# A norm's squares added over partitions by two float32r matmuls, and 1/rms by a root, a reciprocal and a Newton step

## The chip, the cores and the metric

The kernel runs on one core of one Trainium2 chip. The metric is device time in microseconds (us) of one execution, as the median of several runs. The program is one hybrid decoder layer, float32 in and out.

## What is computed

With 256 tokens and a model width of 1024, the part that matters is the second half of the layer:

```
x   = x + mixed @ w_out                     # residual, x is (256, 1024)
h2  = x * rsqrt(mean(x*x over 1024) + 1e-6) * norm_ffn_g
up  = causal_depthwise_conv(h2 @ w_up, conv_w, conv_b)    # 3 taps along tokens
gate, val = split(up, 2)                    # 2816 each
out = x + (silu(gate) * val) @ w_down
```

Ahead of it stand a first norm, eight heads of attention, a pooling branch and two gated branch projections. They are not touched.

## The kernel before

Everything after the projections for q, k and v lies transposed: features on the 128 partitions, the 256 tokens along the row. A feature tile is 128 features, so x has 8 tiles (`xT[:, j, :]`), and the FFN has 22 gate tiles and 22 value tiles.

**Split products.** A float32 matmul is replaced by three float32r ones. Every weight and every activation is split into a high part, rounded by ScalarE (ACT), `high` (L84, L85), and a low part, the difference, made by VectorE (DVE), `low` (L87 to L91). `mm3` (L93) multiplies high by high, high by the activation's low part, and the weight's low part by high. A product of 8 feature tiles is thus 24 matmuls of 128x128 by 128x256.

**Weights.** They come as chunks of 128x2048 floats, in one list (`order`, L102 to L112): up25 is the FFN's tile 0 (one gate tile and one value tile), up26 tile 1, up27 tile 2, up28 tile 3, dn29 two tiles of the down projection, up30 tile 4, up31 tile 5, dn32, and so on. SyncE loads them into 4 buffers. Each chunk is split in two halves of 128x1024: `next_high` (L145) rounds the next half on ACT, `next_low` (L159) makes the difference of an earlier one on DVE, one half behind, and then issues a load. `ahead` (L169) does one of each, and a second time if fewer low halves than `upto` are ready beyond the chunk in use. Each engine takes its instructions in the order in which the code gives them, so where a call of `ahead` stands decides what its half stands behind on ACT and on DVE. The first half of an up chunk holds feature tiles 0 to 3, the second 4 to 7; the third matmul of a feature tile reads the low half.

**The second norm.** After each output tile of `w_out`, `residual` (L588) adds it to x, splits x times the norm's weight into `hhi` and `hlo`, and adds its squares to `ss2` (128 x 256, on POOL, the last one on DVE). The norm's factor is applied after the up projection: `normed` (L630) multiplies a finished tile by `R2`, in which every partition holds 1/rms of all 256 tokens.

The code around the change is L676 to L697. The first two up tiles (up0_0 and up0_1) run over the first 7 feature tiles. Then two matmuls with `ss2` as the weights and a column of ones (L682) put the sums per token on partitions. `rms` (L250) adds epsilon on DVE and takes the power -1/2 on POOL. After the last feature tile of both, two calls of `ahead` and the third up tile (up1_0), `diagonal` (L256) puts the factors on the diagonal of two 128x128 matrices, high and low, and `spread_rms` (L263) multiplies them by `ones_r`, a matrix of ones, which puts every token's factor on all partitions; DVE copies it to `R2`. From there each tile pair goes through `normed`, `taps` (two DVE steps of the convolution), Silu on ACT and the product on POOL; `down` (L654) follows from tile 3 on, three tiles behind.

The line numbers in the profile are those of this kernel; a helper's line stands for all its callers.

Of the kernel before, what the change touches and what calls it, by code (L numbers as in the profile page):

```python
# [8 lines left out]
F32 = mybir.dt.float32  # L9
F32R = mybir.dt.float32r  # L10
AF = mybir.ActivationFunctionType
ALU = mybir.AluOpType
AX = mybir.AxisListType

P = 128
S = 256
NT = S // P
D = 1024
# [12 lines left out]
EPS = 1e-6  # L31
# [20 lines left out]
AHEAD = 4  # L52
FFN_AHEAD = 6
FIRST = 1
HOME = 8
LEAD = 104


# [6 lines left out]
def hybrid_layer_kernel(ctx: ExitStack, tc: tile.TileContext, xq_d, xtok_d, par_d, wkv_d, wpg_d,  # L65
                        wpool_d, wba_d, wbp_d, wout_d, wup_d, wdn_d, out_d):
    nc = tc.nc

    const = ctx.enter_context(tc.tile_pool(name="const", bufs=1))
# [7 lines left out]
    ps2 = pairs.enter_context(tc.tile_pool(name="ps2", bufs=2, space=bass.MemoryType.PSUM))  # L77
    tmp = mixer.enter_context(tc.tile_pool(name="tmp", bufs=2))
# [5 lines left out]
    def high(hi, src, scale=1.0):  # L84
        nc.scalar.activation(hi, src, AF.Copy, scale=scale)  # L85

    def low(lo, hi, src, scale=None):  # L87
        if scale is None:
            nc.vector.tensor_tensor(lo, src, hi.bitcast(F32), ALU.subtract)  # L89
        else:  # L90
            nc.vector.scalar_tensor_tensor(lo, src, scale, hi.bitcast(F32), ALU.mult, ALU.subtract)  # L91
# [53 lines left out]
    def next_high():  # L145
        if at[0] < len(pieces):
            c, sl, first, _ = pieces[at[0]]
            if c - oldest() >= WBUFS:
                return
            at[0] += 1  # L150
            if first:
                moving = order[c][0] in "qkv"
                place = MOVING if moving else 0
                his[c] = whi_p.tile([P, CH + P], F32R, tag="whi", name=f"hi_{order[c][0]}{c}")[:, place:]
                place = MOVING if moving else FAR
                los[c] = wlo_p.tile([P, CH + P], F32R, tag="wlo", name=f"lo_{order[c][0]}{c}")[:, place:]
            high(his[c][:, sl], raw(c, sl))

    def next_low(eager=False):  # L159
        if at[1] < at[0] - STAGGER or at[0] == len(pieces) > at[1] or (at[1] < at[0] and eager):  # L160
            c, sl, _, last = pieces[at[1]]
            at[1] += 1
            low(los[c][:, sl], his[c][:, sl], raw(c, sl))
            if last and order[c][0] != "q":
                load()
# [3 lines left out]
    def ahead(upto=0):  # L169

        next_high()
        next_low()
        if at[1] - sum(p[0] < used[0] for p in pieces) < upto:
            next_high()
            next_low()

    def chunk(name):
        c = used[0]
        used[0] += 1
        spent.update(i for i in range(c) if order[i][0] != "dn")  # L180
        assert order[c][0] == name and all(p[0] > c for p in pieces[at[1]:]), (name, order[c][0])
        return his[c], los[c]


    ones = const.tile([P, P], F32, name="ones")
    nc.vector.memset(ones, 1.0)
    ones_r = const.tile([P, P], F32R, name="ones_r")
# [9 lines left out]
    scrap = const.tile([P, 1], F32, name="scrap")  # L197
# [21 lines left out]

    ident = const.tile([P, P], F32, name="ident")  # L220
    make_identity(nc, ident)
    ss1 = const.tile([P, HOME], F32, name="ss1")[:, 0:NT]
    mhalf = const.tile([P, H], F32, name="mhalf")
    nc.gpsimd.memset(mhalf, -0.5)
    mask = const.tile([P, 3, P], F32, name="mask")
# [18 lines left out]
    R1 = const.tile([P, S], F32, name="R1")  # L244
    rtok1 = const.tile([P, NT], F32, name="rtok1")
    R2 = const.tile([P, S], F32, name="R2")
    rtok2 = const.tile([P, NT], F32, name="rtok2")
    diag = const.tile([P, 2, NT, P], F32R, name="diag")

    def rms(rtok, ss, name):  # L250

        v = const.tile([P, NT], F32, name=f"var_{name}")
        nc.vector.tensor_scalar(v, ss, 1.0 / D, EPS, op0=ALU.mult, op1=ALU.add)
        nc.gpsimd.tensor_tensor(rtok, v, mhalf[:, 0:NT], ALU.pow)

    def diagonal(rtok):  # L256

        for t in range(NT):
            high(diag[:, 0, t, :], ident, rtok[:, t:t + 1])
        for t in range(NT):  # L260
            low(diag[:, 1, t, :], diag[:, 0, t, :], ident, rtok[:, t:t + 1])

    def spread_rms(pb, R):  # L263

        for i in range(2):
            nc.tensor.matmul(pb, ones_r, diag[:, i].rearrange("p t c -> p (t c)"), start=i == 0, stop=i == 1)
        nc.vector.tensor_copy(R, pb)
# [290 lines left out]
    tmp = ctx.enter_context(tc.tile_pool(name="ffn", bufs=2))  # L558
# [18 lines left out]
    hhi = act.tile([P, KD, S], F32R, tag="xhi", name="hhi")  # L577
    hlo = act.tile([P, KD, S], F32R, tag="xlo", name="hlo")
    ss2 = tmp.tile([P, S], F32, tag="ss2", bufs=1, name="ss2")

    def tile_part(w, opers, c, ps, ks):
        hi, lo = w
        oph, opl = opers
        for k in ks:
            sl = slice(k * 256 + c * P, k * 256 + (c + 1) * P)
            mm3(ps[:, 0:S], (hi[:, sl], lo[:, sl]), (oph[:, k, :], opl[:, k, :]), k == 0, k == KD - 1)

    def residual(j, ps):  # L588
        nc.vector.tensor_tensor(xT[:, j, :], ps[:, 0:S], xT[:, j, :], ALU.add)
        g = par[:, C_FFN + j:C_FFN + j + 1]  # L590
        high(hhi[:, j, :], xT[:, j, :], g)
        if j == 0:
            nc.scalar.activation(ss2, xT[:, j, :], AF.Square)
        else:
            s2 = tmp.tile([P, S], F32, tag="s2", name=f"s2_{j}")
            nc.scalar.activation(s2, xT[:, j, :], AF.Square)
            if j < KD - 1:
                nc.gpsimd.tensor_tensor(ss2, ss2, s2, ALU.add)
        if j < KD - 2:
            ahead(AHEAD if j % 2 == 0 else 0)  # L600
        low(hlo[:, j, :], hhi[:, j, :], xT[:, j, :], g)
        if j == KD - 1:
            nc.vector.tensor_tensor(ss2, ss2, s2, ALU.add)

    nc.scalar.activation(scrap, ones[:, 0:1], AF.Silu)
    for b in range(4):
        w = chunk("o")
        ps = [bank(f"ps_out{b}{c}") for c in range(2)]
        if b == 0:

            for ks in (range(KD - 1), range(KD - 1, KD)):
                for c in range(2):
                    tile_part(w, (mh, ml), c, ps[c], ks)
            residual(0, ps[0])
            residual(1, ps[1])
        else:
            for c in range(2):
                tile_part(w, (mh, ml), c, ps[c], range(KD))
                residual(2 * b + c, ps[c])
    ahead()  # L620


    acch, accl = {}, {}

    def taps(u, f, c):
        cw = [par[:, C_CW + j * 2 * KF + f:C_CW + j * 2 * KF + f + 1] for j in range(3)]
        nc.vector.scalar_tensor_tensor(c[:, 1:S], u[:, 0:S - 1], cw[1], c[:, 1:S], ALU.mult, ALU.add)
        nc.vector.scalar_tensor_tensor(c[:, 2:S], u[:, 0:S - 2], cw[0], c[:, 2:S], ALU.mult, ALU.add)  # L628

    def normed(ps, f, name):  # L630

        u = tmp.tile([P, S], F32, tag="u", bufs=4, name=f"u_{name}")
        nc.vector.tensor_tensor(u, ps[:, 0:S], R2, ALU.mult)  # L633
        c = tmp.tile([P, S], F32, tag="cv", bufs=5, name=f"c_{name}")
        cw = par[:, C_CW + 2 * 2 * KF + f:C_CW + 2 * 2 * KF + f + 1]
        nc.scalar.activation(c, u, AF.Identity, scale=cw, bias=par[:, C_CB + f:C_CB + f + 1])
        return u, c

    def gate_done(i, uc):
        taps(uc[0], i, uc[1])  # L640
        nc.scalar.activation(uc[1], uc[1], AF.Silu)

    def value_done(i, g, uc):
        taps(uc[0], KF + i, uc[1])
        nc.gpsimd.tensor_tensor(uc[1], g[1], uc[1], ALU.mult)  # L645
        acch[i] = tmp.tile([P, S], F32R, tag="ah", bufs=LAG + 2, name=f"ah{i}")
        accl[i] = tmp.tile([P, S], F32R, tag="al", bufs=LAG + 2, name=f"al{i}")
        high(acch[i], uc[1])
        return uc[1]
# [27 lines left out]
    ps0 = [bank(f"ps_up0_{c}") for c in range(2)]  # L677
    for c in range(2):
        tile_part(w0, (hhi, hlo), c, ps0[c], range(KD - 1))
    stat = ps2.tile([P, 2, 512], F32, tag="ps2", name="ps_n2")  # L680
    for t in range(NT):
        nc.tensor.matmul(stat[:, 0, t:t + 1], ss2[:, t * P:(t + 1) * P], ones[:, 0:1], start=True, stop=True)  # L682
    rms(rtok2, stat[:, 0, 0:NT], "n2")
    for c in range(2):
        tile_part(w0, (hhi, hlo), c, ps0[c], range(KD - 1, KD))
    for _ in range(2):
        ahead()
    w = chunk("up")
    ps = [bank("ps_up1_0")]
    tile_part(w, (hhi, hlo), 0, ps[0], range(KD))  # L690
    diagonal(rtok2)
    ahead()
    spread_rms(stat[:, 1, 0:S], R2)
    ug = normed(ps0[0], 0, "g0")
    uv = normed(ps0[1], KF, "v0")
    gate_done(0, ug)
    done = value_done(0, ug, uv)  # L697
    for i in range(1, KF):
# [104 lines left out]
```

## Time and profile before

| | us |
|---|---|
| median of 3 runs | 336.04 (335.89 to 336.39) |
| the profiled execution | 336.69 |
| its span, first to last instruction | 334.9 |
| TensorE busy | 330.4 (99%) |
| VectorE busy | 257.4 (77%) |
| ScalarE busy | 201.3 (60%) |
| POOL busy | 87.6 (26%) |

The span is the stretch that the profile shows; the rest of the execution lies around it. In the profile PE is the matmuls, PEld their weight loads, which lie beside other matmuls. Durations of neighbours on PE overlap: the pace is the distance of two starts, not the duration of one. A row of the timeline gives a start, a duration, the engine, the line, and what was written from what; idle time before it stands in brackets with what ended it. Buffer numbers are left out in these names, so `lo_up` is any up chunk's low part. The granted clock of TensorE was 0.999 of full speed over the span.

### The profile page before, as it was taken

To read this page: it belongs to the slowest core of one execution; us is meant where nothing else is said; L and a number is where in the kernel's file an instruction comes from. 1 tells how busy PE (TensorE), PEld (TensorE's weight loads), DVE (VectorE), ACT (ScalarE), POOL (GpSimd) and SP (SyncE) were. 2 spreads that over 40 slices of the span, in tenths; PEclk is the share of its full clock that TensorE was granted. 3 is DMA by queue.
4 is the path that set the end of the run, shared out by engine and by line. 5 is a ranking of instruction groups with operands and counts; after the bars stand their busy time and mean duration, and the time that the engine had idled before them with its cause. 6 is when DMAs were issued, how large, how long until landed. Compare 5 with 4: busy or idle time off the path is not lost.

```text
span 334.9 us, 6726 instructions
## 1 busy us (share of the span) xinstructions
PE 330.4 (99%) x2734; PEld 321.0 (96%) x2734; DVE 257.4 (77%) x409; ACT 201.3 (60%) x325; POOL 87.6 (26%) x100
## 2 busy tenths in 40 slices
PE   8999999999999999999999999999999999999995
PEld 7888899999999999999999999999999999999995
DVE  4839999978776785898998888777778777777644
ACT  5768627654849864677566666555556564646420
POOL 1006893102404034023232312121212121212230
PEclk9999999999999999999999999999999999999999
DMA  7997653464364390573566566463736464551003
GB/s 263 421 416 290 219 183 124 153 252 133 138 232 158 131 342 2 168 248 157 197 241 213 171 245 202 179 250 128 250 130 249 144 236 158 221 174 78 0 2 125
DMA packets 10686, 63.81 MB, mean 191 GB/s; under 512 B 1184, under 2 KB 2336, under 8 KB 3616
## 3 DMA queue, kind: packets, MB, share of 16 engines
q1 hardware_dynamic: 10656, 63.39, 52.3%
q8 instruction: 21, 0.34, 0.4%
q14 instruction: 9, 0.07, 0.1%
HBM read 62.33 MB, written 1.05 MB: 189 GB/s over the span
## 4 chain that ended last, share of the span: by engine, by line
PE 97%; DMA 1%; ACT 0%; DVE 0%; issue 0%
PE ps_up L97 12%; PE ps_up L98 12%; PE ps_up L99 12%; PE ps_d L662 6%; PE ps_d L664 6%; PE ps_d L663 6%; PE ps_g L97 5%; PE ps_g L99 4%; PE ps_g L98 4%; PE ps_q L284 4%; PE ps_v L284 3%; PE ps_k L284 3%; PE ps_out L99 2%; PE ps_out L98 2%; PE ps_out L97 2%; DMA xq<-in_xq 1%
## 5 line engine op out<-in xcount | busy, mean ns | idle before, releaser
L98 PE MATMUL ps_up<-hlo,hi_up 128*128 128x256 f32 x352 | 97.3, 276 | 0.0
L97 PE MATMUL ps_up<-hhi,hi_up 128*128 128x256 f32 x352 | 97.3, 276 | 0.0
L99 PE MATMUL ps_up<-hhi,lo_up 128*128 128x256 f32 x352 | 97.2, 276 | 0.0
L98 PEld LDWEIGHTS ps_up<-hlo,hi_up 128*128 128x128 f32 x352 | 66.1, 188 | 0.1
L97 PEld LDWEIGHTS ps_up<-hhi,hi_up 128*128 128x128 f32 x352 | 66.1, 188 | 0.0
L99 PEld LDWEIGHTS ps_up<-hhi,lo_up 128*128 128x128 f32 x352 | 66.1, 188 | 0.0
L89 DVE TENSOR_TENSOR lo_up<-raw_up,hi_up 128x1024 fp32r<-128x1024 f32 x44 | 55.8, 1271 | 6.5 <-ACT hi_up L85 6.5
L662 PE MATMUL ps_d<-ah,hi_dn 128*128 128x256 f32 x176 | 48.6, 276 | 0.0
L663 PE MATMUL ps_d<-al,hi_dn 128*128 128x256 f32 x176 | 48.6, 276 | 0.0
L664 PE MATMUL ps_d<-ah,lo_dn 128*128 128x256 f32 x176 | 48.6, 276 | 0.0
L645 POOL TENSOR_TENSOR c_v<-c_g,c_v 128x256 f32<-128x256 f32 x22 | 16.2, 737 | 117.5 <-DVE c_v L628 112.1
L85 ACT ACTIVATE hi_up<-raw_up 128x1024 fp32r<-128x1024 f32 x44 | 45.1, 1046 | 0.0
L85 ACT ACTIVATE ah<-c_v 128x256 fp32r<-128x256 f32 x22 | 9.2, 418 | 45.8 <-POOL c_v L645 45.8
L97 PE MATMUL ps_g<-xhi,hi_g 128*128 128x256 f32 x128 | 35.9, 280 | 0.0
L98 PE MATMUL ps_g<-xlo,hi_g 128*128 128x256 f32 x128 | 35.3, 276 | 0.0
L99 PE MATMUL ps_g<-xhi,lo_g 128*128 128x256 f32 x128 | 35.3, 276 | 0.0
L663 PEld LDWEIGHTS ps_d<-al,hi_dn 128*128 128x128 f32 x176 | 33.0, 188 | 0.0
L664 PEld LDWEIGHTS ps_d<-ah,lo_dn 128*128 128x128 f32 x176 | 33.0, 188 | 0.0
L662 PEld LDWEIGHTS ps_d<-ah,hi_dn 128*128 128x128 f32 x176 | 33.0, 188 | 0.0
L89 DVE TENSOR_TENSOR lo_dn<-raw_dn,hi_dn 128x1024 fp32r<-128x1024 f32 x22 | 27.3, 1242 | 0.4 <-ACT hi_dn L85 0.4
L633 DVE TENSOR_TENSOR u_v<-ps_up,R 128x256 f32<-128x256 f32 x22 | 9.3, 421 | 20.5 <-PE ps_up L99 20.5
L669 POOL TENSOR_TENSOR al<-c_v,ah 128x256 fp32r<-128x256 f32 x22 | 21.5, 979 | 11.6 <-ACT ah L85 11.6
(182 smaller groups left out, 804.3 us busy)
## 6 DMA issues: line engine op xcount, KB each, us to landing
raw_up<-in_wup SPq DMA_DIRECT2D x22, 1024.0 KB, 4.8
raw_dn<-in_wdn SPq DMA_DIRECT2D x11, 1024.0 KB, 4.7
raw_g<-in_wpg SPq DMA_DIRECT2D x8, 1024.0 KB, 4.9
raw_o<-in_wout SPq DMA_DIRECT2D x4, 1024.0 KB, 4.8
raw_v<-in_wkv SPq DMA_DIRECT2D x2, 1024.0 KB, 15.7
raw_p<-in_wpg SPq DMA_DIRECT2D x2, 1024.0 KB, 11.3
raw_bp<-in_wbp SPq DMA_DIRECT2D x2, 1024.0 KB, 4.8
raw_ba<-in_wba SPq DMA_DIRECT2D x2, 1024.0 KB, 4.9
```

The costliest lines, as they stand in the source:

```text
L85: nc.scalar.activation(hi, src, AF.Copy, scale=scale)
L89: nc.vector.tensor_tensor(lo, src, hi.bitcast(F32), ALU.subtract)
L97: nc.tensor.matmul(out, sh, mh, start=start, stop=False, **kw)
L98: nc.tensor.matmul(out, sh, ml, start=False, stop=False, **kw)
L99: nc.tensor.matmul(out, sl, mh, start=False, stop=stop, **kw)
L284: nc.tensor.matmul(pt[t], sx[:, k, t * P:(t + 1) * P], wx[:, sl], start=k == 0 and sx is xhi and wx is hi, stop=k == KD - 1 and wx is lo)
L633: nc.vector.tensor_tensor(u, ps[:, 0:S], R2, ALU.mult)
L645: nc.gpsimd.tensor_tensor(uc[1], g[1], uc[1], ALU.mult)
L662: nc.tensor.matmul(o, hi[:, sl], acch[i], start=first, stop=False, skip_group_check=True)
L663: nc.tensor.matmul(o, hi[:, sl], accl[i], start=False, stop=False, skip_group_check=True)
L664: nc.tensor.matmul(o, lo[:, sl], acch[i], start=False, stop=i == KF - 1, skip_group_check=True)
L669: nc.gpsimd.tensor_tensor(accl[i], act_i, acch[i].bitcast(F32), ALU.subtract)
```

## The change

The sum of squares `ss2` is itself split into `sh2` and `sl2`. Two matmuls with `ones_r` as the weights add it over partitions, and the sums stand on all partitions at once. `inverse_root` takes the root on ACT (with the mean and epsilon in its scale and bias), the reciprocal on DVE, and one Newton step there: three more operations of 128x256 and one for the mean. The table of Sqrt is loaded where that of Silu was, and that of Silu after the root. The diagonal matrices, their two matmuls, the copy, and POOL's power of this norm are gone; the first norm keeps them. Three calls of `ahead` become two, the second after `normed`. A small tile holds epsilon beside the first norm's sums.

```diff
--- before.py
+++ after.py
@@ -52,7 +52,7 @@
 AHEAD = 4
 FFN_AHEAD = 6
 FIRST = 1
-HOME = 8
+HOME = 24
 LEAD = 104
 
 
@@ -219,7 +219,9 @@
 
     ident = const.tile([P, P], F32, name="ident")
     make_identity(nc, ident)
-    ss1 = const.tile([P, HOME], F32, name="ss1")[:, 0:NT]
+    small = const.tile([P, HOME], F32, name="small")
+    ss1, eps = small[:, 0:NT], small[:, NT:NT + 1]
+    nc.gpsimd.memset(eps, EPS)
     mhalf = const.tile([P, H], F32, name="mhalf")
     nc.gpsimd.memset(mhalf, -0.5)
     mask = const.tile([P, 3, P], F32, name="mask")
@@ -244,7 +246,6 @@
     R1 = const.tile([P, S], F32, name="R1")
     rtok1 = const.tile([P, NT], F32, name="rtok1")
     R2 = const.tile([P, S], F32, name="R2")
-    rtok2 = const.tile([P, NT], F32, name="rtok2")
     diag = const.tile([P, 2, NT, P], F32R, name="diag")
 
     def rms(rtok, ss, name):
@@ -577,6 +578,8 @@
     hhi = act.tile([P, KD, S], F32R, tag="xhi", name="hhi")
     hlo = act.tile([P, KD, S], F32R, tag="xlo", name="hlo")
     ss2 = tmp.tile([P, S], F32, tag="ss2", bufs=1, name="ss2")
+    sh2 = tmp.tile([P, S], F32R, tag="sh2", bufs=1, name="sh2")
+    sl2 = tmp.tile([P, S], F32R, tag="sl2", bufs=1, name="sl2")
 
     def tile_part(w, opers, c, ps, ks):
         hi, lo = w
@@ -601,8 +604,10 @@
         low(hlo[:, j, :], hhi[:, j, :], xT[:, j, :], g)
         if j == KD - 1:
             nc.vector.tensor_tensor(ss2, ss2, s2, ALU.add)
-
-    nc.scalar.activation(scrap, ones[:, 0:1], AF.Silu)
+            high(sh2, ss2)
+            low(sl2, sh2, ss2)
+
+    nc.scalar.activation(scrap, ones[:, 0:1], AF.Sqrt)
     for b in range(4):
         w = chunk("o")
         ps = [bank(f"ps_out{b}{c}") for c in range(2)]
@@ -621,6 +626,18 @@
 
 
     acch, accl = {}, {}
+
+    def inverse_root(ss, R):
+
+        root = tmp.tile([P, S], F32, tag="root", bufs=1, name="root")
+        v = tmp.tile([P, S], F32, tag="var", bufs=1, name="var")
+        nc.scalar.activation(root, ss, AF.Sqrt, scale=1.0 / D, bias=eps)
+        nc.scalar.activation(scrap, ones[:, 0:1], AF.Silu)
+        nc.vector.tensor_scalar(v, ss, 1.0 / D, EPS, op0=ALU.mult, op1=ALU.add)
+        nc.vector.reciprocal(R, root)
+        nc.vector.scalar_tensor_tensor(v, R, -0.5, v, ALU.mult, ALU.mult)
+        nc.vector.tensor_tensor(v, v, R, ALU.mult)
+        nc.vector.scalar_tensor_tensor(R, v, 1.5, R, ALU.add, ALU.mult)
 
     def taps(u, f, c):
         cw = [par[:, C_CW + j * 2 * KF + f:C_CW + j * 2 * KF + f + 1] for j in range(3)]
@@ -677,22 +694,20 @@
     ps0 = [bank(f"ps_up0_{c}") for c in range(2)]
     for c in range(2):
         tile_part(w0, (hhi, hlo), c, ps0[c], range(KD - 1))
-    stat = ps2.tile([P, 2, 512], F32, tag="ps2", name="ps_n2")
-    for t in range(NT):
-        nc.tensor.matmul(stat[:, 0, t:t + 1], ss2[:, t * P:(t + 1) * P], ones[:, 0:1], start=True, stop=True)
-    rms(rtok2, stat[:, 0, 0:NT], "n2")
+
+    pn = ps2.tile([P, 2, 512], F32, tag="ps2", name="ps_n2")[:, 0, 0:S]
+    for sx in (sh2, sl2):
+        nc.tensor.matmul(pn, ones_r, sx, start=sx is sh2, stop=sx is sl2)
+    inverse_root(pn, R2)
     for c in range(2):
         tile_part(w0, (hhi, hlo), c, ps0[c], range(KD - 1, KD))
-    for _ in range(2):
-        ahead()
+    ahead()
     w = chunk("up")
     ps = [bank("ps_up1_0")]
     tile_part(w, (hhi, hlo), 0, ps[0], range(KD))
-    diagonal(rtok2)
-    ahead()
-    spread_rms(stat[:, 1, 0:S], R2)
     ug = normed(ps0[0], 0, "g0")
     uv = normed(ps0[1], KF, "v0")
+    ahead()
     gate_done(0, ug)
     done = value_done(0, ug, uv)
     for i in range(1, KF):
```

Three places show how the order moves. In the names up27, up28 and so on are the chunks, the last number is a buffer. First DVE, from the sum of squares to the first normed tiles. Before:

```order
L603 TENSOR_TENSOR ss2_1600<-ss2_1600,s2_7_1876 128x256
L89 TENSOR_TENSOR lo_up26_1780<-raw_up26_1659,hi_up26_1779 128x1024
L253 TENSOR_SCALAR var_n2_1933<-ps_n2_1930 128x2
L89 TENSOR_TENSOR lo_up27_1881<-raw_up27_1673,hi_up27_1880 128x1024 x2
L91 SCALAR_TENSOR_TENSOR diag_173<-ident_117,rtok2_172,diag_173 128x128 x2
L89 TENSOR_TENSOR lo_up28_1945<-raw_up28_1713,hi_up28_1944 128x1024
L267 COPY R2_171<-ps_n2_1930 128x256
L633 TENSOR_TENSOR u_g0_1984<-ps_up0_0_1886,R2_171 128x256
L633 TENSOR_TENSOR u_v0_1988<-ps_up0_1_1887,R2_171 128x256
```

The same stretch after the change:

```order
L606 TENSOR_TENSOR ss2_1600<-ss2_1600,s2_7_1878 128x256
L89 TENSOR_TENSOR sl2_1602<-ss2_1600,sh2_1601 128x256
L89 TENSOR_TENSOR lo_up26_1782<-raw_up26_1661,hi_up26_1781 128x1024
L636 TENSOR_SCALAR var_1938<-ps_n2_1934 128x256
L637 RECIPROCAL R2_172<-root_1937 128x256
L638 SCALAR_TENSOR_TENSOR var_1938<-R2_172,var_1938 128x256
L639 TENSOR_TENSOR var_1938<-var_1938,R2_172 128x256
L640 SCALAR_TENSOR_TENSOR R2_172<-var_1938,R2_172 128x256
L89 TENSOR_TENSOR lo_up27_1885<-raw_up27_1675,hi_up27_1884 128x1024
L650 TENSOR_TENSOR u_g0_1979<-ps_up0_0_1890,R2_172 128x256
L650 TENSOR_TENSOR u_v0_1983<-ps_up0_1_1891,R2_172 128x256
L89 TENSOR_TENSOR lo_up27_1885<-raw_up27_1675,hi_up27_1884 128x1024
```

Before, the two halves of up27 and the first of up28 stood ahead of the first normed tile; now one half of up27 does, and its second stands behind that pair.

Second ACT, from the last squares to the first convolution steps. Before:

```order
L596 ACTIVATE s2_7_1876<-xq_82 128x256
L85 ACTIVATE hi_up27_1880<-raw_up27_1673 128x1024 x2
L85 ACTIVATE hi_up28_1944<-raw_up28_1713 128x1024
L85 ACTIVATE diag_173<-ident_117,rtok2_172 128x128 x2
L85 ACTIVATE hi_up28_1944<-raw_up28_1713 128x1024
L636 ACTIVATE c_g0_1986<-u_g0_1984,par_85 128x256
```

After:

```order
L599 ACTIVATE s2_7_1878<-xq_82 128x256
L85 ACTIVATE sh2_1601<-ss2_1600 128x256
L85 ACTIVATE hi_up27_1884<-raw_up27_1675 128x1024
L634 ACTIVATE root_1937<-ps_n2_1934,small_122 128x256
L635 ACT_TABLE_LOAD
L635 ACTIVATE scrap_86<-ones_79 128x1
L85 ACTIVATE hi_up27_1884<-raw_up27_1675 128x1024
L653 ACTIVATE c_g0_1981<-u_g0_1979,par_85 128x256
```

The rounding of up27 now stands behind `sh2`, and its second half behind the root and the table load; both halves of up28 come after the first convolution step.

Third DVE again, around tile 3's normed tiles. Before:

```order
L633 TENSOR_TENSOR u_g3_2153<-ps_up3_0_2128,R2_171 128x256
L89 TENSOR_TENSOR lo_up30_2082<-raw_up30_1884,hi_up30_2081 128x1024
L633 TENSOR_TENSOR u_v3_2189<-ps_up3_1_2164,R2_171 128x256
L627 SCALAR_TENSOR_TENSOR c_g3_2155<-u_g3_2153,par_85,c_g3_2155 128x255
L628 SCALAR_TENSOR_TENSOR c_g3_2155<-u_g3_2153,par_85,c_g3_2155 128x254
L89 TENSOR_TENSOR lo_up31_2158<-raw_up31_1948,hi_up31_2157 128x1024 x2
L89 TENSOR_TENSOR lo_dn32_2231<-raw_dn32_2009,hi_dn32_2230 128x1024
```

After:

```order
L650 TENSOR_TENSOR u_g3_2154<-ps_up3_0_2129,R2_172 128x256
L89 TENSOR_TENSOR lo_up30_2118<-raw_up30_1888,hi_up30_2117 128x1024
L650 TENSOR_TENSOR u_v3_2186<-ps_up3_1_2161,R2_172 128x256
L644 SCALAR_TENSOR_TENSOR c_g3_2156<-u_g3_2154,par_85,c_g3_2156 128x255
L645 SCALAR_TENSOR_TENSOR c_g3_2156<-u_g3_2154,par_85,c_g3_2156 128x254
L89 TENSOR_TENSOR lo_up30_2118<-raw_up30_1888,hi_up30_2117 128x1024
L89 TENSOR_TENSOR lo_up31_2194<-raw_up31_1991,hi_up31_2193 128x1024 x2
```

Before, the half after `u_g3` is the second of up30; now it is the first, and the second stands after tile 3's gate taps, where the first of up31 stood.

## Rows read from the trace of the kernel before

**Rows 1.** the page, part 1: busy time (share of the span) xinstructions

```profile
PE 330.4 (99%) x2734; PEld 321.0 (96%) x2734; DVE 257.4 (77%) x409; ACT 201.3 (60%) x325; POOL 87.6 (26%) x100
```

**Rows 2.** waits of PE, whole span: engine line waited for: us, times, longest

```profile
PE ps_warm L218 <- DVE ones L186: 1.1, 1, 1.1
```

**Rows 3.** waits of DVE between 150 and 180 us, the same columns

```profile
DVE lo_up L89 <- ACT hi_up L85: 0.4, 1, 0.4
DVE c_g L627 <- ACT c_g L636: 0.3, 1, 0.3
```

**Rows 4.** timeline of PE: start us, us, engine line op out<-in xcount

```profile
155.75 0.28 PE L99 MATMUL ps_up<-hhi,lo_up 128*128 128x256 f32 x1
155.87 0.50 PE L682 MATMUL ps_n<-ones,ss 128*128 128x1 f32 x4
...
156.90 0.28 PE L99 MATMUL ps_up<-hhi,lo_up 128*128 128x256 f32 x1
...
159.65 0.28 PE L99 MATMUL ps_up<-hhi,lo_up 128*128 128x256 f32 x1
159.77 0.40 PE L266 MATMUL ps_n<-diag,ones_r 128*128 128x256 f32 x2
...
160.60 0.28 PE L99 MATMUL ps_up<-hhi,lo_up 128*128 128x256 f32 x1
```

**Rows 5.** timeline of DVE, 154 to 164 us, the same columns

```profile
154.37 0.42 DVE L603 TENSOR_TENSOR ss<-ss,s 128x256 f32<-128x256 f32 x1
154.70 1.22 DVE L89 TENSOR_TENSOR lo_up<-raw_up,hi_up 128x1024 fp32r<-128x1024 f32 x1
...
160.90 0.42 DVE L633 TENSOR_TENSOR u_g<-ps_up,R 128x256 f32<-128x256 f32 x1
...
161.99 0.48 DVE L627 SCALAR_TENSOR_TENSOR c_g<-u_g,par,c_g 128x255 f32<-128x255 f32 x1 [0.34 <-ACT c_g L636]
162.51 0.48 DVE L628 SCALAR_TENSOR_TENSOR c_g<-u_g,par,c_g 128x254 f32<-128x254 f32 x1
```

**Rows 6.** timeline of ACT, the same stretch

```profile
154.15 2.94 ACT L85 ACTIVATE hi_up<-raw_up 128x1024 fp32r<-128x1024 f32 x3
...
161.36 0.60 ACT L636 ACTIVATE c_g<-u_g,par 128x256 f32<-128x256 f32 x1 [1.40 <-DVE u_g L633]
```

**Rows 7.** groups of DVE by form: xcount | busy us, mean ns

```profile
L236 DVE TENSOR_SCALAR xhi<-xq 128x256 fp32r<-128x256 f32 x1 | 0.4, 353 | 2.1 <-DMA xq<-in_xq 2.1
...
L89 DVE TENSOR_TENSOR pooll<-pl,poolh 128x256 fp32r<-128x256 f32 x4 | 1.7, 415 | 0.0
...
L469 DVE RECIPROCAL rs<-sums 128x4 f32<-128x4 f32 x4 | 0.7, 179 | 7.0 <-ACT sm L466 7.0
...
L233 DVE RECIPROCAL rcnt<-rcnt 128x16 f32<-128x16 f32 x1 | 0.3, 254 | 1.3 <-POOL rcnt L230 1.3
```

**Rows 8.** groups of ACT by form, the same columns

```profile
L85 ACT ACTIVATE ah<-c_v 128x256 fp32r<-128x256 f32 x22 | 9.2, 418 | 45.8 <-POOL c_v L645 45.8
...
L501 ACT ACTIVATE xq<-xq,par 128x256 f32<-128x256 f32 x16 | 7.2, 497 | 0.0
...
L605 ACT ACT_TABLE_LOAD x1 | 1.3, 1283 | 0.0
```

**Rows 9.** timeline of DVE, 167 to 180 us

```profile
167.19 1.22 DVE L89 TENSOR_TENSOR lo_dn<-raw_dn,hi_dn 128x1024 fp32r<-128x1024 f32 x1
...
175.00 1.71 DVE L89 TENSOR_TENSOR lo_up<-raw_up,hi_up 128x1024 fp32r<-128x1024 f32 x1
...
178.04 1.22 DVE L89 TENSOR_TENSOR lo_up<-raw_up,hi_up 128x1024 fp32r<-128x1024 f32 x1
```

**Rows 10.** timeline of PE, tiles up3_0 and up4_0

```profile
169.78 0.28 PE L99 MATMUL ps_up<-hhi,lo_up 128*128 128x256 f32 x1
...
176.58 0.28 PE L99 MATMUL ps_up<-hhi,lo_up 128*128 128x256 f32 x1
...
177.94 0.28 PE L99 MATMUL ps_up<-hhi,lo_up 128*128 128x256 f32 x1
```

## The prediction, made before the changed kernel ran

> **What bounds the kernel now.** I read the busy table first: TensorE (PE) is busy 99% of the span [rows 1]. PE's own waits come second, and there the reader is to see one line, 1.1 us at the very start [rows 2]: nothing else in 335 us holds the matmuls up. So the time is the sum of the matmuls, and a change pays only with matmuls taken away and costs only if PE is made to wait. Third I read VectorE (DVE) around the norm. Between 150 and 180 us it is named as waiting 0.4 us for a rounded weight half and 0.3 us for a tap [rows 3]; the first of these comes after 179 us, the second just before the taps at 161.99 [rows 5]. From 161.99 to 179.26 DVE is a full queue without a hole. That queue makes the weights' low halves, which PE reads. How early each half is there is the number this prediction turns on.
>
> **PE: what the norm costs.** The old statistics block runs from the matmul at 155.75 to the one at 156.90: 1.15 us [rows 4]. Six ordinary matmuls lie in it; at the pace of 0.1133 us (176.58 to 177.94 is twelve matmuls, 1.36 us [rows 10]) they take 0.68, so the two float32 products, four passes in the trace, cost 0.47. The spreading block, 159.65 to 160.60, is 0.95 for six ordinary matmuls and the two with `ones_r`: 0.27. The change drops both and adds one pair of the second kind at the place of the first. PE gains 0.47 + 0.27 - 0.27 = 0.47 us, if it never waits.
>
> **Does the new pair wait?** The squares' sum ends on DVE at 154.37 + 0.42 = 154.79 [rows 5]. A hand-over between engines is 0.04 (160.90 + 0.42, then ScalarE (ACT) starts at 161.36 [rows 5, 6]). `sh2` on ACT is a 256-column rounding, 0.42 [rows 8]: 154.83 to 155.25. `sl2` on DVE is a 256-column difference, 0.42 [rows 7]: 155.29 to 155.71. PE comes to the pair at 155.87 and to its second half at 155.99, so it does not wait, by a margin of 0.2. But ACT's roundings of up27, which stood at 154.15 [rows 6], move about 1 us back, and DVE has lost 0.46 waiting for `sh2`.
>
> **DVE: when the taps of tile 0 start now.** Same-engine neighbours overlap by about 0.08 (154.37 + 0.42 against 154.70 [rows 5]); a step that needs the one before starts about 0.04 after its end (161.99, 0.48, then 162.51).
> - `lo_up26`, second half, 1.22: 155.63 to 156.85.
> - The pair's sum is complete about 156.3. ACT's root with a bias column costs 0.50 (as the sigmoid of that size [rows 8]; from 0.42 to 0.60, the Identity with two columns [rows 6]): 156.33 to 156.83. `var` waits for the same ACT event and takes 0.35 [rows 7]: 156.87 to 157.22.
> - The reciprocal of 256 columns is not in the trace. Two smaller ones are: 4 columns in 179 ns, 16 in 254 [rows 7]. The line through them is 6.25 ns a column and 154 ns fixed, and the differences of 256 and 1024 columns (415 ns [rows 7], 1.22 us [rows 9]) have nearly that fixed part, 147. So 154 + 256 x 6.25 = 1.75 us. Bounds: 0.42 if it streams like every other operation of 256 columns; 256 x 15.9 ns = 4.1 us if the 254 ns of the larger one were all in its columns. I take 1.75, because both rows and the fixed part fit it. It runs 157.17 to 158.92.
> - Newton, three dependent steps of 0.48, 0.42 and 0.48: to 160.39.
> - `lo_up27` first half, to 161.53; `u_g0` and `u_v0`, about 0.34 each start to start; `lo_up27` second half, to 163.35. The taps start at 163.27, where they started at 161.99 [rows 5]. DVE is 1.28 us later, and nothing behind it is idle that could give this back.
>
> [...]
>
> **The order: one weight half fewer is made ahead.** In the old code three calls of `ahead` stand between the end of the output projection's queue and the taps; in the new one two. The rows in the section on the change show what follows. Each later slot on DVE holds the half that stood one slot earlier: where `lo_up28` second half stood now stands its first, and the slot after `u_g3` holds the first half of `lo_up30` instead of its second. The catch-up inside the down projection comes only after the slot that matters, so `lo_up30` second half now stands where `lo_up31` first half stood.
>
> The old halves were early by little. `lo_up30` second half ended at 175.00 + 1.71 = 176.71 [rows 9]; PE first reads it at 177.94, as the first half at 176.58 [rows 10]: 1.23 us of cover, less than a slot. With PE 0.47 earlier and DVE 1.28 later, and 0.16 from the end of a half to its first matmul (the hand-over and a weight load one pace ahead):
> - `lo_up28` second half ends in the slot of 167.19: 168.41 + 1.28 = 169.69, first use 169.85. PE wants it at 169.78 - 0.47 = 169.31. Wait 0.54.
> - `lo_up30` first half: 176.71 + 1.28 = 177.99, first use 178.15. PE wants it at 176.58 - 0.47 + 0.54 = 176.65. Wait 1.50.
> - `lo_up30` second half, in the slot of 178.04: 179.26 + 1.28 = 180.54, first use 180.70. PE wants it twelve matmuls on, at 178.15 + 1.36 = 179.51. Wait 1.19.
>
> PE waits 3.23 us and gains 0.47: **2.76 us slower**, which is also 180.70 less the old 177.94. Past that point PE is 2.76 late and DVE 1.28, so every later half has more cover than before, and after tile 5 the order of the halves is the old one again. I find no further wait.
>
> **Edits I cost at nothing.** The one extra memset on POOL at the start lies under DVE's 2.1 us wait for x [rows 7]. The root's table replaces Silu's at the same place. The second table load, 1.28 [rows 8], follows the root to 158.1; the half it delays is rounded by about 159.4 and DVE wants it at 162.1; uncovered, it would cost its 1.28. POOL loses the power step, which waits for nobody now. Loads of later weights are issued a slot later, with two to three chunks still ahead; uncovered they would cost up to the same slot, some 3 us.
>
> **Own time and median.** The profiled execution took 336.69 (span 334.9, 1.8 around it), so 339.45 on its own scale. The median of the runs is 336.04, 0.65 below it. I forecast 336.04 + 2.76 = 338.8.
>
> **Rivals.**
> - *The reciprocal streams.* At 0.42 DVE is not late at the taps (1.28 - 1.33), and only the slot shift is left: `lo_up30` second half is first used at 179.37, +1.43, 337.5. For it: every other 256-column row. Against: the two reciprocals. 12%.
> - *The reciprocal is slower*, 8 ns a column: (179 - 147) / 4 from the smaller row with the differences' fixed part. It takes 2.2, 0.45 more: 339.3. [...] For it: that row; against: the larger row gives 6.7. 18%.
> - *Not slower: PE never waits, and the pair is gained.* 336.04 - 0.47 = 335.6. It decides if `lo_up30` second half is there by 177.3, that is 3.2 us before my figure. For it: PE waited for no weight half anywhere before. Against: DVE's queue has no hole there, and the half stands in a later slot by the program's own order. 8%.
> - *More than one cost at once on DVE* (the same operation takes 1.71 in one slot and 1.22 in another [rows 9], and three moved halves at 0.5 more each are 1.5): 340 and above. 5%.
> - The forecast itself, 338.2 to 339.2: 57%.
>
> The range 337.1 to 339.9 takes in the first two rivals and leaves out some 13%. About 0.2%, 0.67 us, is what a measurement can tell from no change. Slower by more: 57 + 18 + 12 + 5 is 92, and I take one off for what I have not seen, 0.91. Within: 0.07, the case that gains 0.47, which is still no change. Faster: 0.02.
>
> **What would show it.** PE's waits should name DVE's `lo_up` three times, about 0.5, 1.5 and 1.2 us, in tiles up3_0 and up4_0, and none later; DVE should show one reciprocal of about 1.75 us and the taps' first step at 163.3; the new pair should follow its neighbour without a gap. I am wrong if PE's waits stay empty, if the reciprocal is near 0.4, or if the loss lies elsewhere, as in a lower granted clock after the waits or in matmuls that read moved tiles at another pace.

## The result, and the profile after

The changed kernel takes 338.82 us (338.44 to 339.17, 6 runs) beside 336.17 for the kernel before on the same chip (335.89 to 336.42, 6 runs): 2.65 us or 0.8% slower, ratio 1.0077 with a 95% interval of 1.0066 to 1.0087. The span of its profiled execution is 337.2 us, 2.3 more than before. This one trace reaches the norm 0.36 us earlier than the one of before (its last sum of squares starts at 154.01 instead of 154.37), so times of the two traces are compared below from that instruction on. The granted clock of TensorE was 1.000 over the span, so the loss is not a slower clock.

The busy table, as in [rows 1]:

```profile
PE 330.6 (98%) x2730; PEld 320.7 (95%) x2730; DVE 259.4 (77%) x411; ACT 203.1 (60%) x327; POOL 87.3 (26%) x100
```

PE is busy as long as before and the span is longer. The waits of PE and of its weight loads (engine line, waited for, us, times and longest) name what holds it up:

```profile
PE ps_up L99 <- DVE lo_up L89: 2.0, 2, 1.2
```

```profile
PEld ps_up L99 <- DVE lo_up L89: 2.7, 3, 1.4
```

In [rows 2] there was nothing between the start and the end. A matmul's record lasts 0.28 us while the next starts after 0.11, so about 0.17 of each wait counts as busy: that is why PE's busy time did not fall by what the change saves, and why the view of PE shows two of the three waits. The timeline of PE shows the three waits, in the tiles that [rows 10] shows without them; columns are the start, the duration, the engine, the line and the operation:

```profile
168.85 0.28 PE L98 MATMUL ps_up<-hlo,hi_up 128*128 128x256 f32 x1
169.23 0.39 PE L99 MATMUL ps_up<-hhi,lo_up 128*128 128x256 f32 x1
169.45 0.28 PE L97 MATMUL ps_up<-hhi,hi_up 128*128 128x256 f32 x1
...
176.06 0.28 PE L98 MATMUL ps_up<-hlo,hi_up 128*128 128x256 f32 x1
177.52 0.38 PE L99 MATMUL ps_up<-hhi,lo_up 128*128 128x256 f32 x1 [1.18 <-DVE lo_up L89]
177.74 0.29 PE L97 MATMUL ps_up<-hhi,hi_up 128*128 128x256 f32 x1
...
178.91 0.28 PE L98 MATMUL ps_up<-hlo,hi_up 128*128 128x256 f32 x1
180.05 0.39 PE L99 MATMUL ps_up<-hhi,lo_up 128*128 128x256 f32 x1 [0.86 <-DVE lo_up L89]
180.27 0.28 PE L97 MATMUL ps_up<-hhi,hi_up 128*128 128x256 f32 x1
```

The distance of starts is 0.11 where nothing is missing. It is 0.38 ahead of the matmul at 169.23, 1.46 ahead of 177.52 and 1.14 ahead of 180.05, so 0.27, 1.35 and 1.03 are lost there; after each of them the next start comes 0.22 later instead of 0.11. That makes 2.65 + 0.33 = 2.98 us. The norm on PE, to be read beside [rows 4]:

```profile
155.39 0.28 PE L99 MATMUL ps_up<-hhi,lo_up 128*128 128x256 f32 x1
155.51 0.28 PE L700 MATMUL ps_n<-sh,ones_r 128*128 128x256 f32 x1
155.63 0.28 PE L700 MATMUL ps_n<-sl,ones_r 128*128 128x256 f32 x1
155.75 0.28 PE L97 MATMUL ps_up<-hhi,hi_up 128*128 128x256 f32 x1
...
156.34 0.28 PE L99 MATMUL ps_up<-hhi,lo_up 128*128 128x256 f32 x1
```

From 155.39 to 156.34 there are the pair and six ordinary matmuls: 0.95, of which 0.27 is the pair's, and no gap. With the old statistics (0.47) gone and the spreading block replaced by this, PE gained 0.47. 2.98 - 0.47 = 2.51 is the change from the norm to tile 4 by this count, and the runs show 2.65 in all.

DVE at the norm, as [rows 5]:

```profile
154.01 0.42 DVE L606 TENSOR_TENSOR ss<-ss,s 128x256 f32<-128x256 f32 x1
154.91 0.43 DVE L89 TENSOR_TENSOR sl<-ss,sh 128x256 fp32r<-128x256 f32 x1 [0.48 <-ACT sh L85]
155.25 1.22 DVE L89 TENSOR_TENSOR lo_up<-raw_up,hi_up 128x1024 fp32r<-128x1024 f32 x1
156.46 0.43 DVE L636 TENSOR_SCALAR var<-ps_n 128x256 f32<-128x256 f32 x1
156.80 1.74 DVE L637 RECIPROCAL R<-root 128x256 f32<-128x256 f32 x1
158.57 0.42 DVE L638 SCALAR_TENSOR_TENSOR var<-R,var 128x256 f32<-128x256 f32 x1
...
159.49 0.42 DVE L640 SCALAR_TENSOR_TENSOR R<-var,R 128x256 f32<-128x256 f32 x1
159.83 1.22 DVE L89 TENSOR_TENSOR lo_up<-raw_up,hi_up 128x1024 fp32r<-128x1024 f32 x1
160.97 0.42 DVE L650 TENSOR_TENSOR u_g<-ps_up,R 128x256 f32<-128x256 f32 x1
...
162.77 0.47 DVE L644 SCALAR_TENSOR_TENSOR c_g<-u_g,par,c_g 128x255 f32<-128x255 f32 x1
```

The reader is to see a queue: the only hole is the 0.48 ahead of `sl`. The old kernel had one of the same length, which [rows 3] leaves out; the waits of DVE between 150 and 180 us in the kernel before have this row too (and 1.2 us for `hhi` ahead of the sum of squares, as after the change):

```profile
DVE var_n L253 <- PE ps_n L682: 0.5, 1, 0.5
```

From the sum of squares to the first tap (the 128x255 step at 162.77) it is now 8.76 us; before it was 161.99 - 154.37 = 7.62. DVE is 1.14 later although it makes three weight halves in this stretch instead of four. The groups of DVE by form give the reciprocal, xcount, busy us and mean ns, beside [rows 7]:

```profile
L637 DVE RECIPROCAL R<-root 128x256 f32<-128x256 f32 x1 | 1.7, 1743 | 0.0
```

Last, the slots of [rows 9] in the changed kernel:

```profile
167.96 1.22 DVE L89 TENSOR_TENSOR lo_up<-raw_up,hi_up 128x1024 fp32r<-128x1024 f32 x1
...
175.76 1.71 DVE L89 TENSOR_TENSOR lo_up<-raw_up,hi_up 128x1024 fp32r<-128x1024 f32 x1
...
178.78 1.22 DVE L89 TENSOR_TENSOR lo_up<-raw_up,hi_up 128x1024 fp32r<-128x1024 f32 x1
```

The first is the second half of up28, the second the first half of up30, the third the second half of up30, which ends at 180.00. PE's matmul at 180.05 starts 0.05 later.

### The profile page after: what moved, and what is told of

It reads as the page before. It is cut to its first block, busy times and chain, and to the rows that moved or that the text cites. A ratio compares the mean times of both kernels' runs of the same rounds, so it can differ in the third digit from the quotient of the medians.

```text
span 337.2 us, 6720 instructions
## 1 busy us (share of the span) xinstructions
PE 330.6 (98%) x2730; PEld 320.7 (95%) x2730; DVE 259.4 (77%) x411; ACT 203.1 (60%) x327; POOL 87.3 (26%) x100
## 3 DMA queue, kind: packets, MB, share of 16 engines
HBM read 62.33 MB, written 1.05 MB: 188 GB/s over the span
## 4 chain that ended last, share of the span: by engine, by line
PE 84%; DVE 10%; ACT 2%; issue 2%; DMA 1%; POOL 0%; POOLq 0%
PE ps_up L99 10%; PE ps_up L98 10%; PE ps_up L97 10%; PE ps_d L680 6%; PE ps_d L679 6%; PE ps_d L681 6%; PE ps_g L97 5%; PE ps_g L98 4%; PE ps_g L99 4%; PE ps_q L285 3%; PE ps_v L285 3%; PE ps_k L285 3%; DVE lo_up L89 3%; DVE hlo L91 2%; DMA xq<-in_xq 1%
## 5 line engine op out<-in xcount | busy, mean ns | idle before, releaser
L89 DVE TENSOR_TENSOR lo_up<-raw_up,hi_up 128x1024 fp32r<-128x1024 f32 x44 | 55.1, 1254 | 6.1 <-ACT hi_up L85 6.1
```

## The experiments

All times are medians beside the kernel before on the same chip (336.15 to 336.17). Each edit is against the changed kernel unless it says otherwise.

**The third call of ahead put back.**

```diff
     tile_part(w0, (hhi, hlo), c, ps0[c], range(KD - 1, KD))
-    ahead()
+    for _ in range(2):
+        ahead()
     w = chunk("up")
```

> The changed kernel with a third call of ahead put back behind the sums over partitions, as before the change. Theory L (late halves: the low half that PE needs last is late by DVE's longer norm and by its later slot together): one more half, 1.14 us, stands ahead of the taps, but lo_up30's second half gets its old slot back, where its first half ended at 177.47 in the changed trace; with 1.14 more it ends at 178.6 instead of 180.0. PE still waits some 1.7 us, at up2_0 for u_g0 and at up4_0 for that half: about 337.4 us. Rival S (the slot alone): PE waits for nothing and only the gain on PE is left, 335.7. Rival R (the reciprocal's chain on DVE alone): unchanged, 338.8. Rival X (something else, such as moved tiles or the new matmuls): unchanged, 338.8.

Measured: 337.39 us, ratio 1.0036 (1.0023 to 1.0049). The waits of PE, and DVE's first tap and the slot behind `u_g3`:

```profile
PE ps_up L97 <- DVE u_g L650: 0.6, 1, 0.6
PE ps_up L99 <- DVE lo_up L89: 0.5, 1, 0.5
```

```profile
163.74 0.48 DVE L644 SCALAR_TENSOR_TENSOR c_g<-u_g,par,c_g 128x255 f32<-128x255 f32 x1
...
176.72 1.71 DVE L89 TENSOR_TENSOR lo_up<-raw_up,hi_up 128x1024 fp32r<-128x1024 f32 x1
```

The tap starts 9.86 us after the sum of squares (153.88), 1.1 later than in the changed kernel, and yet the kernel is 1.4 us faster, since the slot now holds the second half of up30: it ends at 178.43, and only one late half is left. The other wait is for `u_g0`: tile up2_0 is written to the PSUM bank that `u_g0` still has to read. The slot alone cannot be the cause, since PE still waits; nor the reciprocal alone, since the time moved.

**The reciprocal replaced by a copy, order as changed.** This kernel leaves the division out.

```diff
-        nc.vector.reciprocal(R, root)
+        nc.vector.tensor_copy(R, root)
```

> The changed kernel with the reciprocal left out: a copy of the root stands in its place (0.42 us instead of 1.74), the Newton step runs on it. Theory L: everything behind it on DVE moves up by 1.3, so does the last late half, 338.8 - 1.3 = 337.5 us, with PE still waiting in tile up4_0 and no more in up3_0. Rival S (the slot alone): 338.8. Rival R (the reciprocal's chain alone): all of the loss goes, 335.7. Rival X: 338.8.

Measured: 337.20 us, ratio 1.0034 (1.0021 to 1.0047). The waits of PE's weight loads, and on DVE:

```profile
PEld ps_up L99 <- DVE lo_up L89: 1.4, 2, 1.1
```

```profile
157.13 0.28 DVE L637 COPY R<-root 128x256 f32<-128x256 f32 x1
...
161.65 0.48 DVE L644 SCALAR_TENSOR_TENSOR c_g<-u_g,par,c_g 128x255 f32<-128x255 f32 x1
...
177.67 1.22 DVE L89 TENSOR_TENSOR lo_up<-raw_up,hi_up 128x1024 fp32r<-128x1024 f32 x1
```

The copy takes 0.28, so 1.46 us of the queue are gone, and the last late half ends at 178.89 instead of 180.00; from the sum of squares (154.34 and 154.01) it is 1.44 earlier. The time fell by 1.6. Both halves of tile 4 are still late, and tile 3's no more, as expected. What stays is 1.0 us of loss, or 1.5 without the pair's gain of 0.47, with DVE's first tap 0.31 earlier than before the change (7.31 us after the sum of squares instead of 7.62): the later slot costs this much without any delay of the taps.

**Both edits.** The diff is the two above together.

> Both edits: the third call of ahead back, and a copy in place of the reciprocal, which is left out. Theory L: 337.4 - 1.3 = 336.1 us, one short wait of about 0.4 in tile up4_0 or none. Rivals S and R: 335.7, no wait. Rival X: 338.8.

Measured: 335.75 us, ratio 0.9986 (0.9977 to 0.9996). The waits of PE have the one line of [rows 2] and no other. The timeline still shows one matmul that starts 0.20 after its neighbour instead of 0.11, and the next 0.22 behind it:

```profile
177.05 0.28 PE L98 MATMUL ps_up<-hlo,hi_up 128*128 128x256 f32 x1
177.25 0.39 PE L99 MATMUL ps_up<-hhi,lo_up 128*128 128x256 f32 x1
177.47 0.28 PE L97 MATMUL ps_up<-hhi,hi_up 128*128 128x256 f32 x1
```

So one half is still late by a hair, which costs 0.20 of the pair's 0.47; the medians show 0.40 us gained, and the 336.1 expected was 0.35 too high. The time alone would fit rivals S and R (335.7) as well; the two runs above rule those out. This run closes the question of other causes: the pair of matmuls, the split sum, the root, its tables and the moved tiles are all in this kernel, and it is not slower.

**The old norm with two calls of ahead.** Against the kernel before:

```diff
-    for _ in range(2):
-        ahead()
+    ahead()
...
     diagonal(rtok2)
-    ahead()
     spread_rms(stat[:, 1, 0:S], R2)
     ug = normed(ps0[0], 0, "g0")
     uv = normed(ps0[1], KF, "v0")
+    ahead()
```

> The kernel before, with its norm as it was, but with two calls of ahead placed as the change places them: one ahead of up1_0, one behind the first normed pair. Theory L: the factor still comes through POOL and the spreading matmuls, so u_g0 stays at 160.9; the second half of up27 now stands behind u_v0, and the taps start at 162.7 instead of 161.99. lo_up30's second half stands in the slot of 178.04, 0.7 later, and ends at 180.0 instead of 176.71; PE wants it at 177.94: about 2.0 us slower, 338.2. Rival S (the slot alone, DVE not later): 1.4 slower, 337.6. Rivals R and X: 336.2, as before.

Measured: 338.12 us, ratio 1.0059 (1.0042 to 1.0076). DVE's waits, and its taps and the late half:

```profile
DVE diag L91 <- ACT diag L85: 1.0, 1, 1.0
DVE R L267 <- PE ps_n L266: 0.8, 1, 0.8
```

```profile
162.04 0.48 DVE L627 SCALAR_TENSOR_TENSOR c_g<-u_g,par,c_g 128x255 f32<-128x255 f32 x1
...
178.06 1.22 DVE L89 TENSOR_TENSOR lo_up<-raw_up,hi_up 128x1024 fp32r<-128x1024 f32 x1
```

The old factor comes by a long way through POOL and PE, and the halves that filled DVE's time are now behind it: DVE waits 1.0 and 0.8 us and still has the same halves to make. The taps start 8.12 us after the sum of squares (153.92) instead of 7.62. The order alone, without one new instruction, costs 1.97 us.

**ScalarE makes the factor.** The pair stays; root, reciprocal and Newton step go, the table loaded early is that of Ln, and the third call of ahead is back ahead of up1_0, as in the first experiment.

```diff
-        nc.scalar.activation(root, ss, AF.Sqrt, scale=1.0 / D, bias=eps)
...
-        nc.vector.scalar_tensor_tensor(R, v, 1.5, R, ALU.add, ALU.mult)
+        nc.scalar.activation(v, ss, AF.Ln, scale=1.0 / D, bias=eps)
+        nc.scalar.activation(R, v, AF.Exp, scale=-0.5)
```

> The pair of matmuls kept, the factor made by ScalarE alone: exp(-0.5 ln(mean + eps)), no root, no reciprocal, no Newton step on DVE; the table of Ln is loaded early, that of Exp between the two functions (1.28 us), and Silu's where Silu first comes; three calls of ahead at the places of before. Theory L: DVE loses 1.74 + 1.4 + 0.4 us of work, but the second half of up27 is rounded behind the two functions, near 159.3 on the time of the trace before, so the taps start some 0.4 later than before and Silu's table holds up tile 0's product; lo_up30's second half is late by 0.5 or not at all: 335.7 to 336.3. Rival S (the slot alone, as it is restored): 335.7.

Measured: 336.12 us, ratio 0.9995 (0.9986 to 1.0004), no change. One short wait on PE is left, and DVE waits for a rounding that stands behind the exponential on ACT:

```profile
177.32 0.39 PE L99 MATMUL ps_up<-hhi,lo_up 128*128 128x256 f32 x1 [0.30 <-DVE lo_up L89]
```

```profile
DVE lo_up L89 <- ACT hi_up L85: 1.5, 1, 1.5
```

The taps start 8.07 us after the sum of squares, 0.45 later than before the change, as expected.

**The same, with the queue put in order.** Against the one above:

```diff
             high(sh2, ss2)
-            low(sl2, sh2, ss2)
...
     ahead()
+    low(sl2, sh2, ss2)
...
+    for c in range(2):
+        tile_part(w0, (hhi, hlo), c, ps0[c], range(KD - 1, KD))
     for sx in (sh2, sl2):
         nc.tensor.matmul(pn, ones_r, sx, start=sx is sh2, stop=sx is sl2)
+    ahead()
     inverse_root(pn, R2)
-    for c in range(2):
-        tile_part(w0, (hhi, hlo), c, ps0[c], range(KD - 1, KD))
-    for _ in range(2):
-        ahead()
+    ahead()
```

> As e6_ln_exp, with the queue put in order for DVE: the pair of matmuls after the last feature tile (six matmuls later), so that the second half of up26 stands ahead of sl2 and DVE waits for nothing there; both halves of up27 ahead of the logarithm; the third call of ahead behind the first normed pair. Theory L: the factor is there at 159.1, the taps start at 161.2, 0.8 earlier than before, no half is late, PE waits for nothing and keeps the gain of the pair: 336.15 - 0.45 = 335.7. If PE's gain were not what e3_both shows, 336.15.

Measured: 335.59 us, ratio 0.9980 (0.9971 to 0.9990): 0.58 us or 0.2% faster than the kernel before. PE's waits have the one line of [rows 2] and no other. ACT's steps of the factor, and DVE's queue:

```profile
156.23 0.46 ACT L632 ACTIVATE var<-ps_n,small 128x256 f32<-128x256 f32 x1
156.71 1.28 ACT L633 ACT_TABLE_LOAD   x1
158.00 0.42 ACT L633 ACTIVATE R<-var 128x256 f32<-128x256 f32 x1
```

```profile
153.56 0.42 DVE L606 TENSOR_TENSOR ss<-ss,s 128x256 f32<-128x256 f32 x1
...
155.03 0.42 DVE L89 TENSOR_TENSOR sl<-ss,sh 128x256 fp32r<-128x256 f32 x1
...
158.45 0.43 DVE L643 TENSOR_TENSOR u_g<-ps_up,R 128x256 f32<-128x256 f32 x1 [0.67 <-ACT R L633]
...
160.54 0.48 DVE L637 SCALAR_TENSOR_TENSOR c_g<-u_g,par,c_g 128x255 f32<-128x255 f32 x1
...
174.30 1.72 DVE L89 TENSOR_TENSOR lo_up<-raw_up,hi_up 128x1024 fp32r<-128x1024 f32 x1
```

`sl` stands behind a weight half and waits for nothing, the factor is there 4.9 us after the sum of squares, the taps start 6.98 us after it instead of 7.62, and the second half of up30 ends at 176.02. Three places of the order moved at once, so what each of them is worth is not shown.

**The third call behind the first normed pair.**

```diff
     uv = normed(ps0[1], KF, "v0")
-    ahead()
+    for _ in range(2):
+        ahead()
```

> The changed kernel with a third call of ahead, not where it stood before the change but behind the first normed pair, beside the second. Theory L: u_g0 is not delayed, so PE has no wait for it at up2_0, but the low half of up28 now waits on DVE for its rounding, which ACT does only after tile 0's two convolution steps, and ACT's Silu of tile 0 comes a rounding later: lo_up30 comes about as late as with two calls less half a slot, near 338.1. If the count of halves ahead were what matters, and not where they stand, 337.4 as e1_third_ahead.

Measured: 338.06 us, ratio 1.0050 (1.0037 to 1.0064). DVE, with the idle time in brackets:

```profile
163.77 1.23 DVE L89 TENSOR_TENSOR lo_up<-raw_up,hi_up 128x1024 fp32r<-128x1024 f32 x1 [0.65 <-ACT hi_up L85]
164.92 0.48 DVE L644 SCALAR_TENSOR_TENSOR c_g<-u_g,par,c_g 128x255 f32<-128x255 f32 x1
```

As many halves are made ahead as in e1_third_ahead, but the kernel takes 0.67 us more: DVE stands idle 0.65 us for a rounding that ACT does only behind two convolution steps, and the taps start 10.60 us after the sum of squares (154.32) instead of 9.86. Against the changed kernel the extra half still takes back 0.76 us. So where a call stands counts as well as how many there are.

**All kernels in one count.** The first column is the change, in us, of the stretch from the last sum of squares on DVE to PE's last matmul in the traces (176.91 us before). The second adds up, as for the changed kernel, what PE lost in late starts behind the norm, less the 0.47 that the pair gains where it is in the kernel. The third is the difference of the medians.

| kernel | stretch in the trace | late starts less gain | medians |
|---|---|---|---|
| changed | +2.63 | +2.51 | +2.65 |
| e1_third_ahead, third call put back | +1.20 | +1.17 | +1.24 |
| e2_copy, copy for the reciprocal | +1.19 | +1.10 | +1.05 |
| e3_both, both edits | -0.23 | -0.27 | -0.40 |
| e4_before_two, old norm, two calls | +2.00 | +1.92 | +1.97 |
| e6_ln_exp, factor on ScalarE | +0.16 | +0.11 | -0.05 |
| e7_ln_exp_ahead, the same in order | -0.48 | -0.47 | -0.58 |
| e8_third_behind, third call behind | +1.91 | +1.88 | +1.89 |

The first two columns agree within 0.12 us in every kernel, and the medians lie within 0.21 of the first, so late starts and the pair's gain account for the effect in every kernel to about 0.2 us.

## Why the prediction was right, point by point

- **PE gains 0.47.** Right: the pair with six matmuls takes the 0.95 that the spreading block took, and e7_ln_exp_ahead, where nothing is late, has the stretch behind the norm 0.48 shorter (0.58 by the medians).
- **The pair does not wait.** Right, with 0.3 us between the end of `sl` (155.34) and its matmul (155.63), where 0.2 to 0.3 was worked out.
- **The reciprocal, 1.75.** 1743 ns. The line through the two small rows carries to 256 columns, 6.25 ns each and 154 fixed, or 1754 ns; the slower rival (2.2) and the streaming one (0.42) are out. The other new steps were off by little and in both directions: `var` 0.43 for 0.35 (the row that I used, 353 ns in [rows 7], reads SBUF, `var` reads PSUM; whether that makes the difference no run tells), each of the Newton steps 0.42 with a start every 0.46.
- **DVE 1.28 later at the taps.** 1.14. My reading of DVE's waits beside it was incomplete: [rows 3] leaves out 0.5 us at the old statistics and 1.2 us ahead of the sum of squares. The sum does not use them, since it goes from start to start.
- **The three waits, 0.54, 1.50 and 1.19.** 0.38, 1.46 and 1.14, if the slow start after each is counted with it, in the tiles named. In all they are 2.98 where 3.23 was forecast. The hand-over that I put at 0.16 shows as 0.05 ahead of the matmul and 0.11 behind it.
- **No further wait.** Right: no row of PE's waits comes after tile 4.
- **The order and the reciprocal together.** The forecast's rival without the reciprocal's time, with the slot shift alone, was 337.5, or 1.43 slower; with the copy it is 337.20, 1.05 slower, with DVE's taps 0.31 earlier than before where that rival had them 0.05 earlier. The experiments give the share of each: of the 2.65, the copy takes back 1.62 and the third call 1.43; together they take back 3.07, nearly their sum: the loss, and the pair's gain that it had hidden. Neither alone is enough, since with either a half is still later than its cover.
- **Own time and median.** 336.04 + 2.76 = 338.8 against 338.82; the runs of before moved to 336.17, so the difference was 2.65 for a forecast of 2.76. That the totals agree to 0.02 is luck: the base moved up by 0.13 while the difference came out 0.11 smaller. On the scale of the profiled execution 339.45 was forecast and 339.00 came. The mechanism does not rest on either.

What the prediction did not price is the order with the old norm. By e4_before_two it costs 1.97, more than the 1.5 (without the pair's gain) in e2_copy, since there the taps are later too.

## What to carry to other kernels

When a kernel has no waits on its bounding engine, the number to work out for an edit on another engine is the cover: how long each operand is ready before its first use, in the stretch where that engine's queue has no hole. Half a microsecond saved on the bounding engine was lost six times over (0.47 against 2.98 us), because a cover of 1.23 us met a queue that was 1.1 us late and one step behind in its order. The chain did better on the engine that had holes there (ScalarE, idle 1.40 us ahead of its first convolution step in [rows 6]; 335.59 us in e7_ln_exp_ahead against 336.17 before), though only after the calls that fill a wait had been placed anew: without that it drew level with the kernel before (336.12 in e6_ln_exp).

## What the runs showed of the hardware that was not expected

- A copy of 128x256 float32 from SBUF to SBUF on DVE took 0.28 us (157.13 in e2_copy), where the tensor-tensor steps beside it take 0.42 to 0.43 (157.91 to 160.18), the copy from PSUM in the kernel before 0.41 to 0.42 (L267) and a tensor-scalar step from SBUF 0.35 [rows 7].
- A matmul that had waited for its weights is followed by the next start after 0.22 or 0.23 us instead of 0.11, in each of the twelve cases in these traces (177.52 to 177.74 in the changed kernel, 176.80 to 177.03 in e4_before_two).
- The table load took 1.28 us in every place that these traces show (1283 ns in each of four in the changed kernel), and the next instruction on ACT started 0.01 us after it (156.71 and 158.00 in e7_ln_exp_ahead).
- Logarithm and exponential gave 1/rms in 2.2 us on ACT (156.23 to 158.42 in e7_ln_exp_ahead), less than the root, reciprocal and Newton step (155.95 to 159.91 over two engines). A table load of 1.28 us lies within the 2.2, between the two (156.71). None stands right ahead of the logarithm: ACT goes from a rounding to it (154.34, then 156.23), and the program has a logarithm of one column ahead of the output projection. Another, ahead of Silu, follows at 161.62: between 153 and 165 us there are two loads, where the changed kernel has one (156.44).
